# Latent attention with high and low v in one stationary tile, weights divided on GpSimd, scores four tiles ahead, rope rows by DMA and the last product in two parts

## The chip, the cores and the metric

The kernel runs on one core of a Trainium2 chip. The metric is the time of one execution on the device in microseconds (us). A run is timed several times, and the median is given. One further execution is profiled, and every row below comes from it. The engines are TensorE (PE; its weight loads are PEld), VectorE (DVE), ScalarE (ACT), GpSimd (POOL) and SyncE (SP), whose queue issues the DMAs. SBUF is the on-chip memory, PSUM the memory that PE writes its products to.

## The reference

A network of four layers on 512 latent tokens and 256 context tokens of width 1024: Fourier mixing, differential attention, latent attention, Fourier mixing, each followed by an MLP. The change is in the third layer. Cut to what matters there (16 heads, 64 + 32 columns of q and k, 64 of v; 768 keys, and only the 512 latent queries are needed):

```python
def mla_attend(q_nope, q_rope, k_nope, k_rope, v):
    scale = (MLA_NOPE_DIM + MLA_ROPE_DIM) ** -0.5
    s = (einsum("bqhd,bkhd->bhqk", q_nope, k_nope)
         + einsum("bqhr,bkr->bhqk", q_rope, k_rope)) * scale
    p = softmax(s, axis=-1)
    return einsum("bhqk,bkhe->bqhe", p, v)
# mla_mixer: q, k, v by low-rank products of the normed input, the rope part of k shared by all heads,
# q_rope and k_rope rotated; y = concat(heads) @ w_o; x = x + gate * y, then the MLP
```

## The kernel before, in words

All products are made in float32 accuracy from pairs: `split` (L95) rounds a tile to a high part on ACT (L96) and puts the rest, the low part, on DVE (L97); a product is three matmuls, high x high, high x low and low x high (`mm3`, L160). Only PE's order is written by hand: PE executes its instructions in the order of the program text. The other engines' queues are ordered by a scheduler that simulates the program, takes what is ready and prefers what comes first in the text; `tc.high_priority(200)` moves a step forward (the splits of transposed tiles, L799, and the sums into x, L370). Each engine executes its own queue strictly in order. A tile is allocated by a tag with a number of buffers; an instruction that writes a new tile waits until the old tile of its buffer has been read.

The layer (`mla`, L1083) first makes the compressed q and kv (`cqn`, `ckn`), the shared rope rows of k (`krh`, `krl`, 32 rows of 768 columns) and, for four heads at a time, the rope rows of q (`qr_item`, L1180). `kk_rope` (L1170) copies the k rope rows to rows 64 to 96 of one of four key tiles `kkh`, `kkl`; `q_item` (L1220) does the same for the two heads of a pair with the q rope rows (L1230 on ACT, L1231 on DVE).

Then comes a loop over 32 steps c (L1336). A step is 256 queries of one head; eight steps are a group g of four heads. Score tiles are counted by i, two to a step, 128 queries by 768 keys each. `S(i)` (L1269) makes the scores of a tile in six matmuls into a PSUM tile `ps` (tag s, two buffers), takes the row maximum on DVE (L1280), scales it (L1281) and makes the exponential `e` on ACT (L1283; tag e, three buffers). `Tr(i)` (L1286) transposes e on PE, six times 128x128 (L797, in `transpose_g`), into PSUM and splits it to `pth` and `ptl`. `PV(c)` (L1294) multiplies the transposed weights of the step with v in 18 matmuls of 256 columns. Its stationary tile holds 64 columns of v and 64 columns of ones (of zeros for the low part), so that rows of the result hold the sum of the weights; its inverse is made by Ln and Exp on ACT (L1311, L1312), multiplied in on DVE (L1313), and the head's output is split into `oh` and `ol`. The text runs two score tiles ahead: S(0) and S(1), and then in each step Tr(2c), S(2c+2), fill, Tr(2c+1), S(2c+3), fill, PV(c).

`fill` takes other products from a list, about 1.05 us of PE time a call: v of the next group (`v_item`), k and q of the next pair (`k_item`, `q_item`), q rope rows (`qr_item`), and the eight products of the output matrix for the group before (`wo_item`, L1233), each of which ends with a sum into x on DVE (`accum`, L368). Group 3's own eight output products come after the loop, with the steps of the MLP norm behind each (`nm.feed`, L341: a scaled high part on ACT, the low part on DVE, squares on ACT, and a sum `nacc` on POOL, L357). Weights come by `wload` or `gload` on SP's queue into one of two `raw` buffers and are split from there.

Of the kernel before, what the change touches and what calls it, by code (L numbers as in the profile page):

```python
# [44 lines left out]
def body(ctx: ExitStack, tc, a, out):  # L45
# [1037 lines left out]
    def mla(l, h, nm):  # L1083
        T = TT
        with ExitStack() as es:
# [33 lines left out]
            def lat_norm(ps, acc, hl, c0, inv_n, gcol):  # L1119
# [5 lines left out]
                for i, p in enumerate(ps):  # L1125
                    u = qt_("u")[:, :w]
                    nc.vector.scalar_tensor_tensor(u, p, pb[:, gcol + i:gcol + i + 1], r, op0=ALU.mult, op1=ALU.mult)
                    split(hl[i][0][:, c0:c0 + w], hl[i][1][:, c0:c0 + w], u)

            vt = [cp.tile([128, 6, 6, 64], F32R, name=f"vt{q}") for q in range(2)]  # L1130
            zt = sp.tile([128, T], F32, name="zt", tag="e", bufs=3)
            nc.gpsimd.memset(zt[:, :384], 0.0)
            for b in range(2):
                nc.scalar.activation(vt[0][:, :, 3 * b + 1], zt[:, :384].rearrange("p (t e) -> p t e", e=64), AF.Copy, bias=1.0)
                nc.scalar.copy(vt[1][:, :, 3 * b + 1], zt[:, :384].rearrange("p (t e) -> p t e", e=64))
# [11 lines left out]
            lat_norm(pqs, aq, cqn, 0, 1.0 / 256, PB_QG)  # L1147
            akv = sumsq([pkv[:, 0:512]])
            wr = wload(wp, a["mwr"], 256)
            kr = sp.tile([32, T], F32, name="kr", tag="e", bufs=3)  # L1150
            krh, krl = (sp.tile([32, T], F32R, name=n, tag="e", bufs=3) for n in ("krh", "krl"))
# [11 lines left out]
            lat_norm([pkv[:, 0:512]], akv, ckn, 0, 1.0 / 128, PB_KVG)  # L1163
# [6 lines left out]
            def kk_rope():  # L1170
                k_h = hp.tile([96, 776], F32R, name="kkh", tag="h")
                k_l = hp.tile([96, 776], F32R, name="kkl", tag="h")
                nc.scalar.copy(k_h[64:96, :T], rd(krh))
                nc.vector.tensor_copy(k_l[64:96, :T], rd(krl))
# [24 lines left out]
            def v_item(g, t0):  # L1199
# [7 lines left out]
                for b in range(2):  # L1207
                    hi, lo = (q[:, t0:t0 + 2, 2 * b:2 * b + 4:3] for q in vt)
                    split(hi, lo, pv[:, :, 2 * b:2 * b + 2])
# [10 lines left out]
            def q_item(pr):  # L1220
# [3 lines left out]
                for b in range(2):  # L1224
# [5 lines left out]
                    nc.scalar.copy(qh[64:96], rd(qr[hd // 4][0][s]))  # L1230
                    nc.vector.tensor_copy(ql[64:96], rd(qr[hd // 4][1][s]))  # L1231

            def wo_item(g, n, norm=None):  # L1233
                if n == 0:
                    WO[g] = [wload(wp, a["mwo"][2 * g + i]) for i in range(2)]
                p = pt_("u")
                mm3(p, 2, lambda k: kview(WO[g][k], n), lambda k: O[2 * g + k], parts(SL))
                accum(n, 0, SL, p, l, G_A)
                if norm:
                    norm.feed(n)  # L1240
# [28 lines left out]
            def S(i):  # L1269
# [10 lines left out]
                nc.vector.reduce_max(mx, s[:, :T], axis=AX.X)  # L1280
# [195 lines left out]
```

## Time and profile before

| | us |
|---|---|
| median of three runs | 2903.64 |
| lowest and highest of them | 2901.41, 2911.14 |
| the profiled execution | 2903.82 |
| its span, from the first to the last instruction | 2902.0 |
| PE busy in the span | 2756.0 (95%) |
| DVE busy | 1930.2 (67%) |
| ACT busy | 1290.8 (44%) |
| POOL busy | 159.9 (6%) |

The four layers lie behind each other in the span. The loop of the latent attention runs from about 1801 us, where the first row maximum is taken, to 2067 us, where the last PV ends; the output products and the norm follow until about 2090 us. A busy share is the time in which at least one instruction of the engine runs. In rows of groups the number before the arrow is what an instruction writes, the ones behind it what it reads. The granted clock of PE is 0.984 of full speed on average over the span.

### The profile page before, as it was taken

The numbers are of one execution on the slowest core, as the hardware profiler recorded it, in microseconds if no ns is written. First come the engines' busy times: TensorE is split into PE (matmuls) and PEld (weight loads), VectorE is DVE, ScalarE is ACT, GpSimd is POOL, SyncE is SP. The second block draws the span as 40 slices with busy tenths as digits, with TensorE's granted clock in tenths as the row PEclk, the third lists the DMA queues.
The fourth block names the chain that finished last, engine by engine and source line by source line (L and its number), as shares of the span: only waits on it lengthen the run. The fifth ranks groups of instructions, "written<-read, shape, count | busy, mean of one in ns | idle before, by whom it ended". The sixth has DMA issues, their size and how long they took to land.

```text
span 2902.0 us, 39734 instructions
## 1 busy us (share of the span) xinstructions
PE 2756.0 (95%) x15579; PEld 2377.6 (82%) x15579; DVE 1930.2 (67%) x3390; ACT 1290.8 (44%) x2325; POOL 159.9 (6%) x172
## 2 busy tenths in 40 slices
PE   8999999999799989799999998899899999999998
PEld 5788888888788878688888896788788888788887
DVE  7986666558697788875555448888785555664344
ACT  4542222234475656432332236777553334553342
POOL 0110000002110010100000011000100001100001
PEclk9999999999899999999999998999999999999999
DMA  9454333332111111253333210001265551232231
GB/s 319 148 181 131 110 116 104 107 95 82 48 48 45 40 47 39 96 161 114 120 113 116 88 37 32 22 23 37 71 224 175 163 173 55 81 116 95 80 110 51
DMA packets 93531, 291.12 MB, mean 100 GB/s; under 512 B 10624, under 2 KB 14880, under 8 KB 92832
## 3 DMA queue, kind: packets, MB, share of 16 engines
q1 hardware_dynamic: 90784, 285.44, 30.6%
q0 software_dynamic: 2560, 3.15, 0.5%
q8 instruction: 122, 2.00, 0.3%
q14 instruction: 65, 0.53, 0.1%
HBM read 283.29 MB, written 2.11 MB: 98 GB/s over the span
## 4 chain that ended last, share of the span: by engine, by line
PE 79%; DVE 13%; ACT 4%; issue 1%; DMA 1%; POOL 0%; POOLq 0%; SPq 0%; ACTq 0%; DVEq 0%
PE pw L140 70%; PE pu L140 5%; PE ps L140 3%; DVE x L371 2%; PE pu L797 1%; DVE ptl L97 1%; DVE mx L948 1%; DVE wlo L97 1%; DVE hlo L330 1%; DVE nu L328 1%; DVE mx L1280 1%; ACT e L1283 1%; DVE hlo L348 0%; PE pn L140 0%; ACT pth L96 0%
## 5 line engine op out<-in xcount | busy, mean ns | idle before, releaser
L96 ACT CAST whi<-raw 128x1024 fp32r<-128x1024 f32 (+1 forms) x322 | 308.2, 984 | 1064.7 <-PE pw L140 1012.0
L140 PE MATMUL pw<-hhi,wlo 128*128 128x512 f32 (+2 forms) x1680 | 588.0, 350 | 13.0 <-DVE wlo L97 13.0
L140 PE MATMUL pw<-hhi,whi 128*128 128x512 f32 (+2 forms) x1680 | 591.2, 352 | 3.2 <-ACT whi L96 1.5
L140 PE MATMUL pw<-hlo,whi 128*128 128x512 f32 (+2 forms) x1680 | 589.8, 351 | 0.0
L140 PE MATMUL pw<-ahi,whi 128*128 128x512 f32 (+1 forms) x1664 | 569.1, 342 | 0.0
L140 PE MATMUL pw<-alo,whi 128*128 128x512 f32 (+1 forms) x1664 | 567.6, 341 | 0.5 <-DVE alo L97 0.5
L140 PE MATMUL pw<-ahi,wlo 128*128 128x512 f32 (+1 forms) x1664 | 566.6, 340 | 0.0
L371 DVE SCALAR_TENSOR_TENSOR x<-pw,mod,x 128x512 f32<-128x512 f32 (+1 forms) x504 | 302.1, 623 | 283.0 <-PE pw L140 281.8
L97 DVE TENSOR_TENSOR wlo<-raw,whi 128x1024 fp32r<-128x1024 f32 (+1 forms) x322 | 362.2, 1140 | 164.1 <-ACT whi L96 163.5
L140 PEld LDWEIGHTS pw<-hhi,wlo 128*128 128x128 f32 x1680 | 319.4, 190 | 56.7 <-DVE wlo L97 13.6
L140 PEld LDWEIGHTS pw<-hhi,whi 128*128 128x128 f32 x1680 | 318.8, 190 | 47.7 <-ACT whi L96 1.9
L140 PEld LDWEIGHTS pw<-hlo,whi 128*128 128x128 f32 x1680 | 318.7, 190 | 42.4
L140 PEld LDWEIGHTS pw<-ahi,whi 128*128 128x128 f32 x1664 | 315.5, 190 | 37.0 <-issue 0.2
L140 PEld LDWEIGHTS pw<-alo,whi 128*128 128x128 f32 x1664 | 315.5, 190 | 36.2 <-DVE alo L97 0.7
L140 PEld LDWEIGHTS pw<-ahi,wlo 128*128 128x128 f32 x1664 | 315.1, 189 | 36.1
L264 DVE SCALAR_TENSOR_TENSOR raw<-raw,cb 128x1024 f32<-128x1024 f32 x176 | 216.0, 1228 | 117.2 <-DMA raw<-in_modw 115.5
L264 DVE SCALAR_TENSOR_TENSOR junk<-raw,cb 128x1024 bf16<-128x1024 f32 x96 | 117.2, 1220 | 70.6 <-DMA raw<-in_modw 68.4
L97 DVE TENSOR_TENSOR alo<-r,ahi 128x768 fp32r<-128x768 f32 (+2 forms) x134 | 105.8, 792 | 75.1 <-ACT ahi L96 74.8
L307 POOL TENSOR_TENSOR nacc<-nacc,nsq 128x256 f32<-128x256 f32 x70 | 52.9, 755 | 1751.5 <-ACT nsq L306 1751.2
L97 DVE TENSOR_TENSOR ptl<-pu,pth 128x384 fp32r<-128x384 f32 (+1 forms) x208 | 106.2, 539 | 37.5 <-ACT pth L96 36.0
L797 PE MATMUL pu<-ident,e 128*128 128x128 f32 x576 | 89.1, 280 | 21.1 <-ACT e L1283 11.8
L140 PE MATMUL pw<-hhi,g 128*128 128x512 f32 (+2 forms) x384 | 97.8, 337 | 3.9 <-DVE x L371 2.9
(327 smaller groups left out, 4259.4 us busy)
## 6 DMA issues: line engine op xcount, KB each, us to landing
raw<-in_w SPq DMA_DIRECT2D x252, 512.0 KB, 4.1
raw<-in_modw SPq DMA_DIRECT2D x176, 512.0 KB, 3.7
wm<-in_msh SPq DMA_DIRECT2D x32, 256.0 KB, 6.0
raw<-in_fw SPq DMA_DIRECT2D x10, 512.0 KB, 4.3
cb<-scr SPq DMA_DIRECT2D x4, 1024.0 KB, 5.3
raw<-in_dwk SPq DMA_DIRECT2D x16, 256.0 KB, 2.6
raw<-in_dwq SPq DMA_DIRECT2D x16, 256.0 KB, 2.7
raw<-in_dwv SPq DMA_DIRECT2D x16, 256.0 KB, 2.8
```

The costliest lines, as they stand in the source:

```text
L96: nc.scalar.copy(hi, src)
L97: nc.vector.tensor_sub(lo, src, rd(hi))
L140: r = nc.tensor.matmul(o, lhsT, rhs, start=start, stop=stop)
L264: nc.vector.scalar_tensor_tensor(o, m, 1.0, cb[:, v * 1024:(v + 1) * 1024], op0=ALU.mult, op1=ALU.mult, accum_out=mcol(mod[l, ch], v, k))
L307: nc.gpsimd.tensor_tensor(nacc[:, c0:c0 + w], nacc[:, c0:c0 + w], s, op=ALU.add)
L328: nc.vector.scalar_tensor_tensor(u, xs, am, r, op0=ALU.mult, op1=ALU.mult)
L330: nc.vector.scalar_tensor_tensor(lo, u, sh, rd(hi), op0=ALU.add, op1=ALU.subtract)
L371: nc.vector.scalar_tensor_tensor(xs, src, mcol(mod[l, ch], 0 if c0 < SL else 1, n), xs, op0=ALU.mult, op1=ALU.add)
L797: nc.tensor.transpose(t[:, i * 128:(i + 1) * 128], p[:, (k0 + i) * 128:(k0 + i + 1) * 128], ident)
L948: nc.vector.reduce_max(mx, sv, axis=AX.X, negate=True)
L1280: nc.vector.reduce_max(mx, s[:, :T], axis=AX.X)
L1283: nc.scalar.activation(et, s[:, :T], AF.Exp, bias=mx, scale=MLA_SCALE)
```

## The change

- v: the two tiles `vt` (with their columns of ones and zeros) become one tile with v high and v low of a head side by side, 64 columns each, in an order that depends on the head's place in its pair. PV makes 12 matmuls, six with the high and six with the low transposed weights; each gives two sets of 64 rows, one from v high and one from v low. ACT copies one set, and DVE adds the other to it.
- division: the exponential also gives its row sum `li` (`accum_out`), DVE inverts it, and POOL multiplies e by it, in place, before the transposes. The score scale is put into the gain of the compressed q (`qg`), so that the scaling of the maximum goes and the maximum is taken negated.
- scores: four tiles ahead in place of two; tag e has five buffers in place of three. The score tiles keep two PSUM buffers.
- rope rows: the copies to rows 64 to 96 of the q and key tiles become DMAs on SP's queue, forty in all: eight for the keys of four buffers, 32 for the 16 heads.
- last product: in step 30 the list is emptied and the last output weights are loaded and split. After the loop PE makes the first half (heads 12 and 13) of the output products 0 to 3 in the two score buffers, then the last PV, the first half of 4 and 5, and then the second halves, with 6 and 7 whole.

```diff
-                nc.scalar.copy(k_h[64:96, :T], rd(krh))
-                nc.vector.tensor_copy(k_l[64:96, :T], rd(krl))
+                nc.sync.dma_start(rd(k_h)[64:96, :T], rd(krh))
+                nc.sync.dma_start(rd(k_l)[64:96, :T], rd(krl))
...
-                    hi, lo = (q[:, t0:t0 + 2, 2 * b:2 * b + 4:3] for q in vt)
+                    hi, lo = (vt[:, t0:t0 + 2, b::2, q] for q in (b, 1 - b))
...
-                    nc.scalar.copy(qh[64:96], rd(qr[hd // 4][0][s]))
-                    nc.vector.tensor_copy(ql[64:96], rd(qr[hd // 4][1][s]))
-
-            def wo_item(g, n, norm=None):
+                    nc.sync.dma_start(rd(qh)[64:96], rd(qr[hd // 4][0][s]))
+                    nc.sync.dma_start(rd(ql)[64:96], rd(qr[hd // 4][1][s]))
+
+            def wo_load(g):
+                WO[g] = [wload(wp, a["mwo"][2 * g + i]) for i in range(2)]
+
+            def wo_part(p, g, n, k0=0, k1=2):
+                for k in range(k0, k1):
+                    (wh, wl), (oh, ol) = kview(WO[g][k], n), O[2 * g + k]
+                    for i, (u, v) in enumerate(((wh, oh), (wh, ol), (wl, oh))):
+                        mm(p, u, v, k == 0 and i == 0, k == 1 and i == 2)
...
-                nc.vector.reduce_max(mx, s[:, :T], axis=AX.X)
-                nc.vector.tensor_scalar(mx, mx, -MLA_SCALE, None, op0=ALU.mult)
-                et = sp.tile([128, T], F32, name="e", tag="e", bufs=3)
-                nc.scalar.activation(et, s[:, :T], AF.Exp, bias=mx, scale=MLA_SCALE)
+                li = sp.tile([128, 1], F32, name="li", tag="li", bufs=4)
+                nc.vector.reduce_max(mx, s[:, :T], axis=AX.X, negate=True)
+                et = sp.tile([128, T], F32, name="e", tag="e", bufs=5)
+                nc.scalar.activation(et, s[:, :T], AF.Exp, bias=mx, accum_out=li)
+                nc.vector.reciprocal(li, li)
+                nc.gpsimd.tensor_scalar(et, et, li, None, op0=ALU.mult)
...
-                bl = (0, 1, 3, 4)[hd % 4]
-                i = 0
-                for ps in (((vt[0], pth), (vt[1], pth)), ((vt[0], ptl),)):
+                for i, pt in enumerate((pth, ptl)):
                     for kt in range(6):
-                        for vv, pt in ps:
-                            mm(o, vv[:, kt, bl:bl + 2].rearrange("p b e -> p (b e)"), pt[:, kt], i == 0, i == 17)
-                            i += 1
+                        mm(o, vt[:, kt, hd % 4].rearrange("p q e -> p (q e)"), pt[:, kt], i + kt == 0, i + kt == 6)
...
-                nc.scalar.activation(u[s], o[sl], AF.Ln)
-                nc.scalar.activation(u[s], u[s], AF.Exp, scale=-1.0)
-                nc.vector.tensor_mul(u[s], o[s], u[s])
+                nc.scalar.copy(u[s], o[sl])
+                nc.vector.tensor_add(u[s], o[s], u[s])
...
-            st = {0: S(0)}
-            st[1] = S(1)
+            LEAD = 4
+            st = {i: S(i) for i in range(LEAD)}
...
-                    if i + 2 < 2 * NC:
-                        st[i + 2] = S(i + 2)
+                    if i + LEAD < 2 * NC:
+                        st[i + LEAD] = S(i + LEAD)
...
-                PV(c)
+                if c == NC - 2:
+                    while queue:
+                        pop()
+                    wo_load(3)
+                if c < NC - 1:
+                    PV(c)
+
+            ps = []
+            for q in range(2):
+                p = pt_("s")
+                ps.extend((p[:, 0:512], p[:, 512:1024]))
+            for n in range(4):
+                wo_part(ps[n], 3, n, 0, 1)
             ahead_w1(l)
-            while queue:
-                pop()
+            PV(NC - 1)
+            ps.extend(pt_("u") for _ in range(2))
+            for n in range(4, 6):
+                wo_part(ps[n], 3, n, 0, 1)
             for n in range(KT):
-                wo_item(3, n, nm)
+                if n < 6:
+                    wo_part(ps[n], 3, n, 1, 2)
+                else:
+                    ps.append(pt_("u"))
+                    wo_part(ps[n], 3, n)
+                accum(n, 0, SL, ps[n], l, G_A)
+                nm.feed(n)
```

## Rows read from the trace of the kernel before

**Rows 1.** The page, busy us of each engine (share of the span).
```profile
PE 2756.0 (95%) x15579; PEld 2377.6 (82%) x15579; DVE 1930.2 (67%) x3390; ACT 1290.8 (44%) x2325; POOL 159.9 (6%) x172
```

**Rows 2.** Windows: length, then PE, PEld, DVE, ACT, POOL busy (instructions), clock, DMA.
```profile
1801.00:1873.00 72.00, 60.96 (x382) 53.43 (x380) 60.88 (x122) 50.76 (x98) 4.14 (x3) 0.93 0.07 23
1873.00:1939.00 66.00, 64.50 (x427) 57.41 (x428) 54.75 (x111) 48.09 (x97) 0.00 (x0) 1.00 0.05 17
1939.00:2006.00 67.00, 64.62 (x426) 57.18 (x425) 56.78 (x115) 49.43 (x99) 0.00 (x0) 1.00 0.07 24
2006.00:2066.00 60.00, 56.02 (x377) 49.84 (x378) 48.27 (x100) 42.45 (x87) 0.00 (x0) 1.00 0.13 45
...
2075.00:2090.00 15.00, 12.38 (x65) 10.29 (x65) 14.52 (x23) 10.40 (x23) 11.95 (x7) 1.00 0.02 5
```

**Rows 3.** Waits, 1800 to 2090: total us, times, longest.
```profile
ACT e L1283 <- DVE mx L1281: 35.8, 33, 2.1
...
PE pu L797 <- ACT e L1283: 11.8, 9, 2.7
```

**Rows 4.** Chain of work, 2044 to 2095: start, us, what.
```profile
2056.42 1.06 PE ps L140 x6
...
2059.45 2.15 PE pu L140 x18
```

**Rows 5.** Groups of DVE, 1801 to 2066: busy us, mean ns, idle before.
```profile
L97 DVE TENSOR_TENSOR ol<-nu,oh 64x256 fp32r<-64x256 f32 x30 | 12.4, 415 | 0.6
...
L97 DVE TENSOR_TENSOR wlo<-raw,whi 128x1024 fp32r<-128x1024 f32 x6 | 7.2, 1214 | 0.0
...
L1231 DVE CAST ql<-qrl 32x512 fp32r<-32x512 f32 x14 | 5.9, 420 | 0.4
...
L1174 DVE CAST kkl<-krl 32x768 fp32r<-32x768 f32 x2 | 1.1, 552 | 0.1
```

**Rows 6.** Tile nu in the layer: count, ns min/median/max.
```profile
L1312 ACT ACTIVATE nu<-nu x32: 407/416/421, 1817.4 to 2068.2; 64x256 f32<-64x256 f32 x32
```

**Rows 7.** Tile e, accumulator readout in the layer before: count, ns min/median/max.
```profile
L949 ACT ACTIVATION_READ_ACCUMULATOR e<-ps,mx x64: 187/193/219, 762.9 to 1164.1; 128x1 f32 x64
```

**Rows 8.** DVE's waits in the layer before: total us, times, longest.
```profile
DVE li L950 <- ACT e L949: 5.8, 18, 0.9
```

**Rows 9.** Groups of POOL, whole span: busy us, mean ns, idle before.
```profile
L357 POOL TENSOR_TENSOR nacc<-nacc,nsqw 128x768 f32<-128x768 f32 x7 | 16.4, 2350 | 152.7 <-ACT nsqw L356 140.3 <-ACT hhi L96 12.4
L357 POOL TENSOR_TENSOR nacc<-nacc,big 128x768 f32<-128x768 f32 x7 | 13.3, 1895 | 78.4 <-ACT big L356 68.3 <-ACT hhi L96 9.9
...
L839 POOL CAST kl<-big 64x768 fp32r<-64x768 f32 x4 | 3.4, 862 | 0.2
```

**Rows 10.** Timeline of DVE and POOL, 1184 to 1203: start, us.
```profile
1184.70 0.47 DVE L348 SCALAR_TENSOR_TENSOR hlo<-x,am,hhi 128x256 fp32r<-128x256 f32 x1
...
1186.19 2.07 DVE L348 SCALAR_TENSOR_TENSOR hlo<-x,am,hhi 128x256 fp32r<-128x256 f32 x1
...
1186.14 1.84 POOL L357 TENSOR_TENSOR nacc<-nacc,big 128x768 f32<-128x768 f32 x1 [68.09 <-ACT big L356]
```

**Rows 11.** Timeline of DVE and POOL behind the loop: start, us.
```profile
2078.20 0.75 DVE L371 SCALAR_TENSOR_TENSOR x<-pu,mod,x 128x512 f32<-128x512 f32 x1
...
2077.58 12.86 POOL L357 TENSOR_TENSOR nacc<-nacc,nsqw 128x512 f32<-128x512 f32 x7 [243.49 <-ACT hhi L96]
```

**Rows 12.** DMA issues, whole span: count, KB each, us to landing.
```profile
kh<-kh POOLq DMA_DIRECT2D x16, 64.0 KB, 2.3
```

**Rows 13.** Waits of SP's queue, 1700 to 2100: total us, times, longest.
```profile
SPq L116 <- DVE wlo L97: 126.3, 8, 47.0
```

**Rows 14.** Timeline, first transposes: start, us, idle before.
```profile
1804.35 1.54 PE L797 MATMUL pu<-ident,e 128*128 128x128 f32 x6 [2.72 <-ACT e L1283]
```

**Rows 15.** Timeline, last PV and the first sum with the norm: start, us.
```profile
2065.34 1.68 PE L140 MATMUL pu<-pth,vt 128*128 128x256 f32 x12 [0.25 <-ACT pth L96]
...
2074.09 0.75 DVE L371 SCALAR_TENSOR_TENSOR x<-pu,mod,x 128x512 f32<-128x512 f32 x1 [0.59 <-PE pu L140]
```

More of the change, by code (lines that the diff above doesn't have):

```diff
@@ L1126, in lat_norm @@
                     u = qt_("u")[:, :w]
-                    nc.vector.scalar_tensor_tensor(u, p, pb[:, gcol + i:gcol + i + 1], r, op0=ALU.mult, op1=ALU.mult)
+                    nc.vector.scalar_tensor_tensor(u, p, gcol[:, i:i + 1], r, op0=ALU.mult, op1=ALU.mult)
                     split(hl[i][0][:, c0:c0 + w], hl[i][1][:, c0:c0 + w], u)
[L1130 to L1135, printed above, removed]
+            vt = cp.tile([128, 6, 4, 2, 64], F32R, name="vt")
+            qg = cp.tile([128, 2], F32, name="qg")
+            nc.vector.tensor_scalar(qg, pb[:, PB_QG:PB_QG + 2], MLA_SCALE, None, op0=ALU.mult)
             ckn = [[cp.tile([128, T], F32R, name=f"ckn{q}") for q in range(2)]]
@@ L1146, in mla @@
             mm3(pkv, KT, lambda k: kview(wkv, k), hk, [(0, 512)])
-            lat_norm(pqs, aq, cqn, 0, 1.0 / 256, PB_QG)
+            lat_norm(pqs, aq, cqn, 0, 1.0 / 256, qg)
             akv = sumsq([pkv[:, 0:512]])
             wr = wload(wp, a["mwr"], 256)
-            kr = sp.tile([32, T], F32, name="kr", tag="e", bufs=3)
-            krh, krl = (sp.tile([32, T], F32R, name=n, tag="e", bufs=3) for n in ("krh", "krl"))
+            kr = sp.tile([32, T], F32, name="kr", tag="e", bufs=5)
+            krh, krl = (sp.tile([32, T], F32R, name=n, tag="e", bufs=5) for n in ("krh", "krl"))
             def kr_part(c0, w):
@@ L1162, in mla @@
             kr_part(0, 512)
-            lat_norm([pkv[:, 0:512]], akv, ckn, 0, 1.0 / 128, PB_KVG)
+            lat_norm([pkv[:, 0:512]], akv, ckn, 0, 1.0 / 128, pb[:, PB_KVG:])
             pkc = pt_("u")[:, :256]
@@ L1229, in q_item, with wo_item @@
                     s = slice(32 * (hd % 4), 32 * (hd % 4) + 32)
-                    nc.scalar.copy(qh[64:96], rd(qr[hd // 4][0][s]))
-                    nc.vector.tensor_copy(ql[64:96], rd(qr[hd // 4][1][s]))
-            def wo_item(g, n, norm=None):
+                    nc.sync.dma_start(rd(qh)[64:96], rd(qr[hd // 4][0][s]))
[7 more added lines that the diff above has]
+                        mm(p, u, v, k == 0 and i == 0, k == 1 and i == 2)
+            def wo_item(g, n):
                 if n == 0:
-                    WO[g] = [wload(wp, a["mwo"][2 * g + i]) for i in range(2)]
+                    wo_load(g)
                 p = pt_("u")
-                mm3(p, 2, lambda k: kview(WO[g][k], n), lambda k: O[2 * g + k], parts(SL))
+                wo_part(p, g, n)
                 accum(n, 0, SL, p, l, G_A)
-                if norm:
-                    norm.feed(n)
             def v_items(g):
```

2 lines of the change are left out of this document (1 added, 1 removed).

## The prediction

> **What bounds the kernel now.** I began with the page: TensorE (PE) is busy 95% of the span [rows 1], but that is a mean over four layers, and the change touches only the latent attention layer, from about 1801 us (first score tile) to 2090 us (first product of the MLP behind it). So I cut that stretch by the groups of the attention loop: 32 steps c, eight for each group g of four heads [rows 2]. In g=1 and g=2 PE is busy 64.5 of 66 and 64.6 of 67 us, VectorE (DVE) 54.8 and 56.8, ScalarE (ACT) 48 to 49, GpSimd (POOL) nothing: PE is the bound, and DVE is second at 83 to 85%. In g=0 both PE and DVE stand at 61 of 72 us: there the loop waits back and forth between them. In g=3 PE has 56.0 of 60. Behind the loop, in 2075 to 2090, DVE is busy 14.5 of 15 us: the sums and the MLP norm are DVE's. Then the waits: PE waits 11.8 us in nine places for a softmax tile e, and ACT, which makes e, waits 35.8 us for the row maximum from DVE [rows 3]. So two things can be gained: PE time in the steady groups, and DVE time where PE waits for DVE.
>
> **The change part by part.** The sum is made against the profiled execution, 2903.82 us with a span of 2902.0; the median of the three runs, 2903.64, is the same within 0.2.
>
> *High and low v side by side.* Before, each PV ran 18 matmuls of 256 columns in 2.15 us [rows 4], 0.119 us each. Now the stationary tile holds v high in one half and v low in the other, so 12 do. That takes 6 x 0.119 = 0.72 us from each of 32 steps: 22.9 us of PE, 5.7 a group. All of it lies on PE's own queue.
>
> *Division.* Before, a row of ones gave the sum, and each step paid Ln and Exp on ACT and a multiply on DVE. Now a copy takes Ln's place and an add the multiply's, of the same shapes, so I price them alike; the second ACT operation, 0.416 us [rows 6], goes, 32 x 0.416 = 13.3 us of ACT. In exchange each of the 64 exponentials reads out its accumulator, 0.193 us in the layer before [rows 7], 12.4 us of ACT. Zero for ACT, which is not the bound. On DVE a reciprocal of one column replaces the scaling of the maximum, one column too: zero. But it stands behind an exponential on DVE's in-order queue, and the next subtraction for a transposed tile, which PE's PV waits for, is queued behind it. The layer before runs the same pattern, maximum, exponential, reciprocal, and its DVE waited 5.8 us in 18 places [rows 8]: from below zero, from above 6 us, and I leave it to the share that a stretch can reach.
>
> *The multiply on POOL.* No row shows this form. From below, a one-input cast of 768 columns took 0.862 us; from above, two-input adds of 128x768 took 1.895 and 2.350 [rows 9]. It has one tensor input, so I take 1.0 us, near the cast. As latency it fits: POOL gets 64 us of work in 240. Its cost is what it does to DVE. A subtraction of 128x256 with two SBUF inputs took 0.47 us alone and 2.07 us when it started 0.05 us behind a POOL add of 1.84 us: it waited to the end of the POOL operation [rows 10]. A DVE sum that reads PSUM and one SBUF tile took its usual 0.75 us in the middle of seven POOL adds in a row [rows 11]: it was not held. In the loop the maximum and the subtractions of the transposed tiles read PSUM; with two SBUF inputs there are 52 operations (30 ol and 6 wlo [rows 5], two wlo that move in, and by the code 8 g and 6 in the q rope). If POOL is busy 64 x 1.0 / 240 = 27% of the time, each loses 0.27 x 0.5 us on average: 7 us of DVE over the loop, 1.8 a group. By the ends: 0.86 us gives 5 us, 1.9 us gives 26, 2.35 us gives 39.
>
> The Trainium skill ("SBUF — State Buffer", section "Who interferes with whom") says that DVE and GpSimd share a port pair as an exclusive lock: a DVE instruction with two SBUF inputs contends with a GpSimd instruction that reads SBUF, and one with at most one SBUF input, outside the two-port modes, does not. The trace agrees with both halves [rows 10, 11]. It speaks against the division's place: the sum without any lock would be 7 us of DVE smaller.
>
> *Rope rows by DMA.* This takes 14 casts of 0.42 us (ql) and two of 0.55 us (kkl) from DVE in the loop [rows 5], 7 us, and as many from ACT. Forty DMAs go to SP's queue. An SBUF-to-SBUF copy of 64 KB took 2.3 us to land [rows 12]. SP is a queue with long stalls: a weight load there waited up to 47 us for a free raw buffer [rows 13], and anything behind it waits too. I cost the DMAs at zero in the loop: in program order each pair's DMAs stand ahead of the next weight load, their source is ready from the first steps, and each head is asked for two to four score tiles after its q product. If that cover is gone, one pair waits 2.3 us plus what blocks SP. At the start they are exposed: the first rope rows land some 2.3 us after their source, where a copy took 0.6, but DVE and ACT lose the eight casts of the first four heads that stood around it. I take zero there, from -1 to +3.
>
> *Four tiles ahead.* PE issues scores 2 and 3 before the first transpose. But there are still two score buffers in PSUM, so S(i+4) needs the exponential of i+2 to be done. Before, T(i), the transposes of e, needed it two tiles after S(i); now S(i+2) needs it two tiles after S(i) plus one T: the 11.8 us of waits for e can come back as waits for the score buffer. What the lead does buy is room for the accumulator, the reciprocal and POOL behind the exponential, and at the start and the end: PE's 2.72 us idle before the first transpose [rows 14] gets two score tiles' work, and the last tiles no longer wait for an exponential. I give the lead no more than about 1 us at each end.
>
> *Last product in two parts.* The remaining two products of wo2 move into g=3 (12 matmuls of 512 columns, 2.8 us at the 1.06 us that 2304 score columns took [rows 4]); so do the split of the last weights (two wlo of 1.2 us [rows 5]) and two sums of 0.75 us [rows 15] on DVE. Before, from the start of the last PV (2065.34) to the first sum that went through the norm (2074.09) there were 8.75 us [rows 15]. Now: 12 first-part matmuls 2.8 us, of which some 0.5 lie in the wait for the last split; PV 1.43; the chain copy, add, cast, subtraction 1.6 us plus 0.4 of gaps, partly beside two more first parts; the second part 0.7 and a hand-over of 0.3: 6.7 us. I take a gain of 1.7, for the weight split may be late. Behind it the eight sums and norm steps are DVE's 15 us as before.
>
> **The sum by stretch** [rows 2]. For each I take the new busy times and divide the larger by a share that the stretch can reach: 0.96 in g=1 and g=2 (PE has 0.965 to 0.977 now, but DVE will stand closer), 0.95 in g=3, 0.88 in g=0 (0.85 now).
> g=0: PE 61.0 - 5.7 = 55.3; DVE 60.9 - 2.8 (casts) + 1.8 (lock) = 59.9, so 68.1 for 72: -3.9.
> g=1: PE 64.5 - 5.7 = 58.8; DVE 54.8 - 1.7 + 1.8 = 54.9; 61.3 for 66: -4.7.
> g=2: PE 64.6 - 5.7 = 58.9; DVE 56.9; 61.4 for 67: -5.6.
> g=3: PE 56.0 - 5.0 + 2.8 = 53.8; DVE 48.3 - 0.9 + 2.4 + 1.5 + 1.8 = 53.1; 56.6 for 60: -3.4.
> Tail: -1.7. Together -19.3 us: 2903.8 - 19.3 = 2884.5, forecast 2884.
>
> **The rivals.**
> *PE alone decides.* If DVE always has its results ready, the full 22.9 us, most of the 11.8 us of waits and the tail's 1.7 come back, less the 2.8 moved: about -33 us, 2871. For it: PE is over 96% busy in two groups. Against it: DVE at 90% and more beside it.
> *The lock takes half.* If the multiply runs like the two-input add of 1.9 us, DVE gets 26 us for 7, 6.5 a group: 73.4, 62.1, 64.2 and 60.8 us, 4.5 less than before in all, and the tail: -6 us, 2898. For it: POOL's only measured operations of this width and all 128 partitions are the slow ones.
> *Slower by the same lock.* At 2.35 us each, the third POOL row, 9.8 a group come onto DVE: 77.2, 65.5, 67.7 and 64.3 us, +9.7, less the tail 1.7: 2912. It begins to be slower at about 2.1 us a multiply.
> *Rope rows come late.* If a pair's DMAs stand behind a waiting load in SP's order, the loop stops for them: four or five pairs at 2 to 3 us eat half of the gain, 2894. Against it: program order, above.
>
> **How the numbers follow.** A difference of 0.3% (8.7 us) is about what a measurement of this kernel can tell from no change. Chances: forecast 0.55 (2874 to 2895), PE alone 0.15, lock half 0.18, lock slower 0.07, late rope 0.05. Faster than 2895 lie nearly all of the forecast, PE alone, and some of lock half and late rope: 0.73; same 0.17; slower 0.10 (lock slower and the top of lock half). The range leaves out the lower half of PE alone and the slow lock: 2868 to 2902.
>
> **What would show it.** Right: 384 PV matmuls in the layer where 576 were; DVE over 90% busy in g=1 to g=3 and g=0 the longest group; PE's waits for e replaced by waits at the score tiles; POOL multiplies of about 1 us; a few ol and wlo of over 0.8 us; the first sum of the last product some 7 us after the last transposes. Wrong: POOL multiplies near 2 us, ol means over 0.7 us, PE waiting for a DMA into qh or kkh, or DVE clearly under 85% with PE still idle, which would mean that a chain that I priced at zero (accumulator, reciprocal, POOL) sets the pace.

## The result and the profile after

| | before | after |
|---|---|---|
| median, timed side by side (us) | 2904.82 (2901.41 to 2911.14) | 2880.76 (2879.58 to 2881.57) |
| span of the profiled execution (us) | 2902.0 | 2879.8 |

The ratio is 0.9914, with a 95% interval of 0.9899 to 0.9929: 24 us less by the medians, 22.2 by the two profiled spans. The forecast was 2884, with a range of 2868 to 2902.

The page gives the busy times of the engines. PE has 19.6 us and 192 matmuls less than before [rows 1], DVE 5 us less, and POOL 144 us more:

```profile
PE 2736.4 (95%) x15387; PEld 2356.3 (82%) x15387; DVE 1925.4 (67%) x3371; ACT 1269.4 (44%) x2333; POOL 303.9 (11%) x235
```

To see where the time went, both traces are cut at the same events: first score tile, PV(0), PV(8), PV(16), PV(24), the last PV (each by the start of its first matmul), and the statistic of the MLP norm behind the layer. The columns are those of [rows 2]: length, busy time of PE, PEld, DVE, ACT and POOL, PE's granted clock, DMA. First the kernel before:

```profile
1798.50:1813.82 15.32, 12.13 (x50) 10.11 (x49) 10.43 (x22) 10.20 (x20) 0.00 (x0) 0.71 0.01 2
1813.82:1880.15 66.33, 58.42 (x393) 51.65 (x392) 58.01 (x119) 48.55 (x97) 4.14 (x3) 0.97 0.08 25
1880.15:1947.54 67.39, 64.74 (x428) 57.31 (x427) 57.15 (x115) 49.79 (x100) 0.00 (x0) 1.00 0.07 24
1947.54:2014.71 67.17, 64.78 (x429) 57.32 (x428) 56.95 (x115) 49.59 (x99) 0.00 (x0) 1.00 0.07 24
2014.71:2065.34 50.63, 47.88 (x327) 42.94 (x325) 39.19 (x81) 34.29 (x70) 0.00 (x0) 1.00 0.12 43
2065.34:2094.09 28.75, 24.72 (x127) 20.68 (x127) 23.07 (x36) 14.44 (x30) 12.39 (x7) 0.94 0.15 48
```

and the changed kernel:

```profile
1797.57:1813.13 15.56, 14.24 (x62) 11.69 (x61) 10.68 (x22) 10.37 (x23) 10.12 (x5) 0.73 0.20 46
1813.13:1873.06 59.93, 51.17 (x345) 44.85 (x343) 57.09 (x114) 44.02 (x102) 42.13 (x20) 1.00 0.12 35
1873.06:1934.79 61.73, 58.46 (x378) 51.63 (x379) 56.84 (x111) 45.89 (x103) 36.16 (x17) 1.00 0.12 35
1934.79:1996.27 61.48, 58.31 (x380) 51.52 (x379) 56.65 (x111) 45.48 (x103) 36.17 (x17) 1.00 0.16 45
1996.27:2045.33 49.06, 46.07 (x297) 40.59 (x295) 42.09 (x82) 32.36 (x74) 24.84 (x12) 1.00 0.06 20
2045.33:2072.03 26.70, 20.75 (x98) 16.61 (x97) 18.63 (x30) 12.32 (x27) 11.23 (x7) 0.88 0.32 115
```

| stretch | before | after | difference | forecast |
|---|---|---|---|---|
| ahead of the first score tile | 1798.50 | 1797.57 | -0.9 | 0 |
| to PV(0) | 15.32 | 15.56 | +0.2 | 0 |
| PV(0) to PV(8), nearly g=0 | 66.33 | 59.93 | -6.4 | -3.9 |
| PV(8) to PV(16), g=1 | 67.39 | 61.73 | -5.7 | -4.7 |
| PV(16) to PV(24), g=2 | 67.17 | 61.48 | -5.7 | -5.6 |
| PV(24) to the last PV, g=3 | 50.63 | 49.06 | -1.6 | -3.4 |
| last PV to the statistic | 28.75 | 26.70 | -2.0 | -1.7 |
| behind it | 807.91 | 807.77 | -0.1 | 0 |

The forecast's stretches are cut up to some 8 us earlier than these, so a row is compared loosely, the sums strictly: -19.3 forecast, -22.2 found. Of g=0's gain up to 1.7 us is not the change's: before, PE was granted 1.2 GHz for 3.4 us there (the clock column says 0.97), after it was at 2.4 GHz throughout. In the last stretch it is the other way: 1.2 GHz for 3.4 us before and 6.6 us after. At the two ends the rows don't hold the same work: with the new lead the row to PV(0) has two more score tiles and g=3 two fewer. With the lead alone (below) these two rows took 18.74 and 48.45 us. g=1 and g=2 stand at full clock in both and are the clean measure. There PE was busy 96% of the time before and is busy 95% now; DVE went from 85% to 92%.

The waits from 1795 to 2090 us, longest first (total, times, longest). ACT still waits for the maximum [rows 3], PE no longer waits for e at its transposes but at the score tiles, and DVE waits 8.0 us for the accumulator. A wait of PE stands in these rows twice, once for the weight load (PEld) and once for the matmul (PE), so the two are not added: the matmuls waited 6.6 us for e, where before they waited 11.8 [rows 3].

```profile
ACT e L1288 <- DVE mx L1286: 27.6, 32, 1.8
...
PEld ps L140 <- ACT e L1288: 8.4, 7, 1.9
DVE li L1289 <- ACT e L1288: 8.0, 21, 0.6
...
PE ps L140 <- ACT e L1288: 6.6, 6, 1.6
...
PE ps L140 <- DVE x L371: 2.0, 2, 1.2
```

The groups of POOL and DVE in the loop (busy us, mean ns): the multiply takes 2282 ns, more than twice the 1.0 us of the sum, and yet ol, a DVE operation with two SBUF inputs, takes 464 ns on average where it took 415 [rows 5].

```profile
L1290 POOL TENSOR_SCALAR e<-e,li 128x768 f32<-128x768 f32 x64 | 145.6, 2282 | 93.4 <-DVE li L1289 74.5 <-PE pu L140 12.2 <-ACT g L96 3.8
...
L97 DVE TENSOR_TENSOR ol<-nu,oh 64x256 fp32r<-64x256 f32 x30 | 13.9, 464 | 0.4
...
L97 DVE TENSOR_TENSOR wlo<-raw,whi 128x1024 fp32r<-128x1024 f32 x8 | 9.8, 1234 | 0.1
```

The timeline shows why. An ol that started 0.08 us behind a multiply took 1.10 us: it ran 0.42 us from 1921.68 on, so it was let go 0.76 us after the multiply's start, though the multiply went on for another 1.44 us. An ol that started 0.88 us into another multiply took its usual 0.42. Of the 32 ol in the layer only two started in the first 0.76 us of a multiply, and each took 1.10 us; the 20 that started later in one, from 0.88 us on, took 0.40 to 0.47 us. The rows of the two examples:

```profile
1921.00 1.10 DVE L97 TENSOR_TENSOR ol<-nu,oh 64x256 fp32r<-64x256 f32 x1
...
1920.92 2.20 POOL L1290 TENSOR_SCALAR e<-e,li 128x768 f32<-128x768 f32 x1
...
1863.65 0.42 DVE L97 TENSOR_TENSOR ol<-nu,oh 64x256 fp32r<-64x256 f32 x1
...
1862.77 2.21 POOL L1290 TENSOR_SCALAR e<-e,li 128x768 f32<-128x768 f32 x1
```

### The profile page after: what moved, and what is told of

Read it like the earlier page. It is cut to its first block, busy times and chain, and to the rows that moved or that the text cites. A ratio compares the mean times of both kernels' runs of the same rounds, so it can differ in the third digit from the quotient of the medians.

```text
span 2879.8 us, 39661 instructions
## 1 busy us (share of the span) xinstructions
PE 2736.4 (95%) x15387; PEld 2356.3 (82%) x15387; DVE 1925.4 (67%) x3371; ACT 1269.4 (44%) x2333; POOL 303.9 (11%) x235
## 4 chain that ended last, share of the span: by engine, by line
PE 78%; DVE 14%; ACT 4%; DMA 2%; issue 2%; POOL 1%; POOLq 0%; SPq 0%; ACTq 0%; DVEq 0%
PE pw L140 69%; PE pu L140 4%; PE ps L140 3%; DVE x L371 1%; DVE ptl L97 1%; PE pu L797 1%; DVE wlo L97 1%; DVE mx L948 1%; ACT e L1288 1%; DVE mx L1286 1%; DVE nu L328 1%; DVE hlo L330 1%; PE pn L140 0%; DVE hlo L348 0%; DMA raw<-in_w 0%
## 5 line engine op out<-in xcount | busy, mean ns | idle before, releaser
L140 PE MATMUL pw<-hhi,wlo 128*128 128x512 f32 (+2 forms) x1680 | 587.1, 349 | 12.5 <-DVE wlo L97 12.5
L140 PEld LDWEIGHTS pw<-hhi,wlo 128*128 128x128 f32 x1680 | 318.4, 190 | 56.2 <-DVE wlo L97 13.1
L1290 POOL TENSOR_SCALAR e<-e,li 128x768 f32<-128x768 f32 x64 | 145.6, 2282 | 93.4 <-DVE li L1289 74.5
```

Source lines behind the costliest of these rows:

```text
L140: r = nc.tensor.matmul(o, lhsT, rhs, start=start, stop=stop)
L1290: nc.gpsimd.tensor_scalar(et, et, li, None, op0=ALU.mult)
```

## The experiments

Times are medians, with the ratio to the kernel before, which was run on the same chip in the same set, and its 95% interval. Since these differ by up to 0.15% either way, readings of 1 to 5 us go by the stretches of the traces: the changed kernel was run twice with a profile, and PV(8) to PV(16) took 61.73 and 61.77 us, PV(16) to PV(24) 61.48 and 61.52.

### Six matmuls back into each PV

```diff
-                for i, pt in enumerate((pth, ptl)):
+                for i, pt in enumerate((pth, pth, ptl)):
...
-                        mm(o, ..., pt[:, kt], i + kt == 0, i + kt == 6)
+                        mm(o, ..., pt[:, kt], i < 2 and kt == 0, i != 1 and kt == 5)
```

> The changed kernel with six matmuls of 256 columns put back into each PV: the six with the high transposed weights are issued twice, the second time from a fresh start, so the result is the same and PE has 18 matmuls a step as before. Nothing else differs. Theory A (PE sets the pace in the loop, and the gain is the six matmuls): 32 x 0.72 = 22.9 us come back, 2900 to 2906 us, and DVE's busy share in the loop falls from 92% to about 84%. Rival B (DVE, at 92%, or a chain through it sets the pace, and the matmuls lie beside its work): 10 us or less come back, 2881 to 2891 us.

2898.53 us, ratio 0.9973 (0.9963 to 0.9983). Against the second run of the changed kernel (below) 15.6 us by the medians; in the traces, from the first score tile to the statistic, 286.95 us for 274.46: 12.5. (The profiled execution, 2891.61 us, was the fastest of the eight. Its stretch to PV(0) was 1.3 us shorter, with PE at 1.2 GHz for 2.3 us of it, for 8.4 in the changed kernel; from PV(0) on it took 13.8 us more.) g=1 and g=2 of this run:

```profile
1873.25:1938.42 65.17, 63.47 (x426) 57.16 (x427) 56.41 (x111) 45.32 (x103) 35.62 (x17) 1.00 0.12 33
1938.42:2003.59 65.17, 63.47 (x427) 57.15 (x427) 56.41 (x111) 45.27 (x103) 35.62 (x17) 1.00 0.15 43
```

Neither theory: 3.4 and 3.7 us of 5.7 come back. PE is now busy 97% and DVE 87%. PE's busy time rises by 5.1 us a group, less than the 5.7 that the spacing of the matmuls' starts gives. Read from the other end, this kernel has before's matmuls and takes 65.2 us for 67.3: 2.1 us of a group's gain of 5.7 come from the rest of the change, 3.6 from the matmuls. This holds for the six taken away last; the new v alone, in the kernel before, was not tried.

### Score tiles two ahead

```diff
-            LEAD = 4
+            LEAD = 2
```

> The changed kernel with score tiles two ahead in place of four. From the end of a tile's scores the weights need the maximum 0.95, the exponential 0.90, its accumulator 0.20, the reciprocal 0.16 and the multiply 2.21 us, with hand-overs about 4.8 us. At two ahead PE has one transpose, one score tile, a call of fill and half a PV to do in between, about 3.2 us. Theory A (the lead hides the slow multiply): PE waits for POOL some 1.2 to 1.8 us at each of 62 tiles, 75 to 110 us, 2955 to 2990 us. Rival B (with two score buffers PE waits for the exponential in any case, so the lead hides little): within 5 us of the changed kernel, 2878 to 2886 us.

2931.91 us, ratio 1.0086 (1.0071 to 1.0101): 51 us slower than the changed kernel. The waits of its loop (again on the weight loads and on the matmuls), and g=1:

```profile
PEld pu L797 <- POOL e L1290: 53.2, 34, 4.7
...
PE pu L797 <- POOL e L1290: 44.6, 32, 4.5
...
1888.65:1961.38 72.73, 63.04 (x378) 54.40 (x379) 56.61 (x111) 45.91 (x103) 35.05 (x16) 0.95 0.11 30
```

PE waits for POOL at its transposes, of which the changed kernel shows nothing. Theory A, with a smaller price: 11.0 us more in g=1 for 16 tiles, 0.7 us a tile where 1.2 to 1.8 were expected. Part of it is the clock: from PV(0) to the last PV PE was at 1.2 GHz for 40.9 us (6.8 in g=1), in the changed kernel never. By an estimate from these times, half of them at most was lost: up to 20 of the 51 us, and up to 3.4 of the 11.0.

### The lead alone, in the kernel before

```diff
-            st = {0: S(0)}
-            st[1] = S(1)
+            st = {i: S(i) for i in range(4)}
...
-                    if i + 2 < 2 * NC:
-                        st[i + 2] = S(i + 2)
+                    if i + 4 < 2 * NC:
+                        st[i + 4] = S(i + 4)
```

> The kernel before with one part of the change alone: score tiles four ahead, with five buffers for e. Theory A (as predicted: two score buffers tie S(i+2) to the exponential two tiles back, so waits for e come back as waits for a score buffer, and only the start and the end gain): 0 to 3 us less, 2900 to 2904 us. Rival B (the lead by itself frees PE of its waits for e): up to 12 us less, 2892 us.

2906.6 us, ratio 0.9998 (0.9988 to 1.0007): no difference. PV(8) to PV(24) takes 134.4 us for 134.6. The lead by itself is worth nothing in the time; it is the condition under which a multiply of 2.2 us can stand behind the exponential.

### The division with two tensor inputs on POOL

```diff
-                nc.gpsimd.tensor_scalar(et, et, li, None, op0=ALU.mult)
+                nc.gpsimd.tensor_tensor(et, et, li.to_broadcast([128, T]), op=ALU.mult)
```

> The changed kernel with the division on POOL as an operation of two tensors: e times the inverse sums, read as a second input of 768 columns with stride zero. The product is the same. In the trace of the changed kernel a DVE operation with two SBUF inputs that started just behind a POOL multiply was released 0.76 us after the multiply's start; behind a POOL add of two tensors it was 1.65 us, nearly the add's end. Theory A (the lock lasts as long as POOL reads, by its number of inputs): POOL operations of 1.9 to 2.4 us, DVE operations with two SBUF inputs held up to 1.6 us, mean of the 64x256 subtraction ol from 0.46 to 0.7 us or more, and 5 to 20 us more in all, 2886 to 2900 us. Rival B (the lock plays no part in this loop, whatever POOL reads): ol stays under 0.55 us and the time within 3 us of the changed kernel.

2886.74 us, ratio 0.9932 (0.9917 to 0.9947). The multiply became faster, 1516 ns for 2282, and ol slower, 610 ns. An ol 0.05 us behind a multiply took 1.70 us: it was let go at 1840.29, only 0.14 us ahead of the multiply's end:

```profile
L1290 POOL TENSOR_TENSOR e<-e,li 128x768 f32<-128x768 f32 x64 | 96.5, 1516 | 140.4 <-DVE li L1289 107.8 <-PE pu L140 13.3 <-PE pu L797 11.0
...
L97 DVE TENSOR_TENSOR ol<-nu,oh 64x256 fp32r<-64x256 f32 x30 | 18.3, 610 | 0.4
...
1839.01 1.70 DVE L97 TENSOR_TENSOR ol<-nu,oh 64x256 fp32r<-64x256 f32 x1
...
1838.96 1.47 POOL L1290 TENSOR_TENSOR e<-e,li 128x768 f32<-128x768 f32 x1
...
1872.38:1935.15 62.77, 58.44 (x379) 51.63 (x379) 57.96 (x111) 45.93 (x103) 23.91 (x16) 1.00 0.11 34
```

g=1 and g=2 take 1.0 us more each, with 1.1 us more of DVE busy in each; the first score tile to the statistic takes 278.77 for 274.46. The total is at the lower end of theory A, with intervals that overlap those of the changed kernel; the multiply (1.9 to 2.4 expected) and the mean of ol (0.7 or more) came out below it. So a lock that lasts nearly as long as the operation costs about 1 us a group here, though less than theory A said.

### Rope rows by copies again

```diff
-                    nc.sync.dma_start(rd(qh)[64:96], rd(qr[hd // 4][0][s]))
-                    nc.sync.dma_start(rd(ql)[64:96], rd(qr[hd // 4][1][s]))
+                    nc.scalar.copy(qh[64:96], rd(qr[hd // 4][0][s]))
+                    nc.vector.tensor_copy(ql[64:96], rd(qr[hd // 4][1][s]))
```

(and the same for the key rows)

> The changed kernel with the rope rows copied again, high rows on ACT and low rows on DVE, in place of the forty DMAs. Theory A (DVE at 92% of the loop hands PE its inputs, so DVE time counts now): the four casts of 0.42 us that come back to DVE in each of g=1 and g=2 cost 1 to 1.7 us a group, 3 to 6 us in all, 2884 to 2887 us. Rival B (PE sets the pace and the copies lay beside it): within 1.5 us of the changed kernel.

The changed kernel, run again beside this and the next two:

> The changed kernel itself, timed beside the following ones on the same chip so that they have a common measure. Both theories: 2878 to 2884 us, and from PV(8) to PV(24) 123.2 us as in its first profile.

It took 2882.93 us, ratio 0.9921 (0.9906 to 0.9936); the copies 2888.01 us, ratio 0.9936 (0.9921 to 0.9951). The intervals overlap. The stretches to PV(0), g=0, g=1 and g=2 with the copies:

```profile
1798.35:1815.50 17.15, 14.72 (x62) 11.89 (x61) 13.13 (x28) 13.01 (x27) 9.70 (x5) 0.70 0.01 1
1815.50:1878.33 62.83, 53.81 (x344) 46.95 (x342) 57.85 (x117) 47.17 (x106) 42.42 (x20) 0.95 0.07 22
1878.33:1940.96 62.63, 58.57 (x379) 51.58 (x379) 59.21 (x116) 48.49 (x107) 37.54 (x17) 1.00 0.10 30
1940.96:2002.38 61.42, 58.83 (x381) 51.59 (x379) 57.36 (x115) 47.53 (x107) 35.62 (x17) 1.00 0.12 35
```

Against the changed kernel these are +1.6, +2.9, +0.9 and -0.1 us. The 2.9 of g=0 can't be taken as the copies' cost: PE was granted 1.2 GHz for 6.8 us of it here (0.95 in the column) and never in the changed kernel. Of the 1.6 at the start up to 0.9 may be the clock as well (10.2 us at 1.2 GHz for 8.4). What is left is 0.7 to 1.6 us at the start, 0.9 us in g=1 and nothing in g=2. Neither theory holds as stated: the DMAs seem to gain a little, and the exact size stays open.

### The last product whole

```diff
-                if c == NC - 2:
-                    while queue:
-                        pop()
-                    wo_load(3)
-                if c < NC - 1:
-                    PV(c)
...
+                PV(c)
             ahead_w1(l)
...
+            while queue:
+                pop()
             for n in range(KT):
+                wo_item(3, n)
                 nm.feed(n)
```

> The changed kernel with the last output product as before: its weights are loaded after the last PV, and the eight products come whole behind it. Theory A (the division of the last product in two parts takes some 2 us from the stretch behind the last PV and adds the wait for the late weights, 1.2 us, ahead of it): 0.5 to 3 us slower, 2881 to 2884 us, and from the start of the last PV to the statistic of the norm 28 to 29 us where the changed kernel has 26.7. Rival B (the chain of the sums, the norm steps and POOL's sums of squares sets the end whatever the order of the products): that stretch is 26.7 us or less, and the total is the same or lower.

2880.28 us, ratio 0.9916 (0.9899 to 0.9932), beside 0.9921 of the changed kernel: no difference by the medians. The traces, both with 6.6 us at 1.2 GHz in the last stretch, tell more. First this run, PV(24) to the last PV and the last PV to the statistic, then its first sum with the norm (DVE) and its sums of squares (POOL):

```profile
1994.29:2037.32 43.03, 40.84 (x272) 36.14 (x270) 37.28 (x76) 29.69 (x71) 25.17 (x12) 1.00 0.09 27
2037.32:2066.57 29.25, 25.23 (x120) 21.10 (x121) 23.08 (x36) 14.03 (x29) 12.37 (x7) 0.89 0.28 96
...
2045.55 0.75 DVE L371 SCALAR_TENSOR_TENSOR x<-pu,mod,x 128x512 f32<-128x512 f32 x1 [0.59 <-PE pu L140]
...
2049.06 12.84 POOL L357 TENSOR_TENSOR nacc<-nacc,nsqw 128x512 f32<-128x512 f32 x7 [13.10 <-ACT hhi L96]
```

then the changed kernel, the last transposes on PE, the first sum and the sums of squares:

```profile
2042.19 0.44 PE L797 MATMUL pu<-ident,e 128*128 128x128 f32 x2 [1.19 <-DVE ptl L97]
...
2049.52 0.75 DVE L371 SCALAR_TENSOR_TENSOR x<-ps,mod,x 128x512 f32<-128x512 f32 x1 [0.82 <-PE ps L140]
...
2053.84 11.70 POOL L357 TENSOR_TENSOR nacc<-nacc,nsqw 128x512 f32<-128x512 f32 x7 [15.86 <-ACT nsqw L356]
```

The stretch ahead of the last PV is 6.0 us shorter than in the changed kernel (43.03 for 49.06), the one behind it 2.55 longer (29.25 for 26.70): the division in two parts costs 3.5 us net. For the first sum it does what it should: last PV to first sum 4.2 us in place of 8.2. But the twelve first-part matmuls (2.8 us), the two products of wo2 (2.8 us) and the weight splits now stand ahead of the last PV, on PE's path, where the splits hold up the last transposes by 1.19 us. Behind the last PV such work had stood beside DVE's and POOL's: from the first sum on, POOL's seven sums of squares run one behind the other, 12.84 us here and 11.70 there, DVE's norm steps are held beside them (a 128x2 subtraction of 0.15 us took up to 1.23 in the changed kernel), and PE's first MLP products wait for those. And the divided form has a wait of its own, 2.0 us in the rows above (PE ps <- DVE x): the second parts of products 1 and 3, which share a score buffer with 0 and 2, were begun only when the sums of those were done. Theory A is right on the stretch behind the last PV, theory B on the total.

### The low part of the head outputs on POOL

```diff
-                split(oh[s, c0:c0 + 256], ol[s, c0:c0 + 256], u[s])
+                h_, l_ = oh[s, c0:c0 + 256], ol[s, c0:c0 + 256]
+                nc.scalar.copy(h_, u[s])
+                (nc.gpsimd if c < 30 else nc.vector).tensor_tensor(l_, u[s], rd(h_), op=ALU.subtract)
```

> The changed kernel with the low part of the head outputs (the 64x256 subtraction, 0.46 us, 30 of 32) moved from DVE to POOL. DVE loses 3.7 us of 56.8 a group, and its two-input operations with it; POOL gets some 0.8 us each behind its multiplies. Theory A (PE's waits in the loop are DVE's load): PE comes closer to its 58.4 us a group, 1 us or more less in each of g=1 and g=2, 3 to 6 us in all, 2875 to 2878 us. Rival B (PE waits for chains in a fixed order, not for DVE's load): within 1.5 us of the changed kernel; slower if POOL's queue delays the multiplies.

2875.65 us, ratio 0.9898 (0.9884 to 0.9913). g=1 and g=2, and the group of the moved subtraction:

```profile
1870.84:1930.17 59.33, 58.08 (x379) 51.67 (x379) 52.96 (x103) 45.20 (x103) 41.27 (x26) 1.00 0.13 37
1930.17:1989.48 59.31, 58.08 (x378) 51.67 (x378) 52.95 (x103) 45.22 (x103) 40.88 (x25) 1.00 0.17 49
...
L1318 POOL TENSOR_TENSOR ol<-nu,oh 64x256 fp32r<-64x256 f32 x30 | 23.0, 765 | 15.0 <-ACT oh L1317 14.0
```

2.4 and 2.2 us less a group, with PE 98% busy and DVE 89%. PE's matmuls are the same. Theory A: in the changed kernel time on DVE, 3.9 us a group less here, kept PE from its work. The lock on ol, which goes too, is too small for it (1.5 us in the whole loop). Whether DVE's load as such counts, or only the place of ol in its queue, this edit can't tell apart. The other stretches are within 0.3 us of the changed kernel, but for the one to PV(0), 1.3 us shorter with PE at 1.2 GHz for 2.0 us in place of 8.4.

### The two improvements together

The last two edits in one kernel.

> The changed kernel with the low part of the head outputs on POOL, and with the last output product whole behind the last PV. Theory A (the two act in different stretches, the first in g=1 and g=2, the second in g=3 and behind): the loop gives 6.3 + 3.5 = 9.8 us less in the profile than the changed kernel, 2870 to 2873 us. Rival B (both take the same slack of DVE): only the larger of the two, 2875 to 2877 us.

2870.25 us, ratio 0.9873 (0.9859 to 0.9888): the fastest of all. In the trace the first score tile to the statistic takes 264.78 us, 9.7 less than in the changed kernel; the two alone gave 6.2 and 3.4. Of the 9.7 and of the 6.2, 1.3 lie ahead of PV(0), where the clock differed as in the run before; from PV(0) on the gains are 8.4, 4.9 and 3.4 us. Theory A: they add up. Its g=1:

```profile
1872.06:1931.40 59.34, 58.07 (x378) 51.67 (x378) 52.94 (x103) 45.26 (x103) 41.24 (x26) 1.00 0.14 37
```

The same with the two-input division:

> As the run with the head outputs' low part on POOL and the last product whole, and with the division on POOL as an operation of two tensors (1.47 us, but it held the DVE subtraction ol up to its end). Theory A (the 1.0 us a group that the two-input form cost was the lock on ol, and ol is now off DVE): g=1 and g=2 take 59.3 us as without it, total within 1.5 us of that run. Rival B (the cost lay elsewhere): g=1 and g=2 again take about 1 us more, 60.3 us, and the total is 3 to 5 us above it.

2873.78 us, ratio 0.9880 (0.9862 to 0.9899).

```profile
1877.23:1936.54 59.31, 58.05 (x378) 51.65 (x379) 52.94 (x103) 45.25 (x103) 29.21 (x24) 1.00 0.13 37
1936.54:1995.87 59.33, 58.05 (x378) 51.65 (x378) 52.95 (x103) 45.28 (x104) 29.19 (x24) 1.00 0.13 37
```

g=1 and g=2 are the 59.3 us of the run without it: the 1.0 us a group is gone once ol is off DVE. Theory A there. That it was the lock on ol fits the row of ol above (0.15 us more on seven or eight a group); but DVE has more spare time here, in which a hold of another operation would not show. The median is 3.5 us higher, as rival B had it, but the intervals overlap and the two can't be told apart; g=0 took 4.3 us more in the profile, with PE at 1.2 GHz for 13.7 us of it, against 3.4.

And with the six matmuls put back:

> As the run with the head outputs' low part on POOL and the last product whole, with the six matmuls put back into each PV. Theory A (a group takes PE's time or what DVE allows, whichever is more; with DVE at 89% of 59.3 us PE alone decides): each group takes the full 5.7 us more, 65.0 us in g=1 and g=2, total 2892 to 2896 us. Rival B (part of PV's matmuls lies beside other work in any case): 3.6 us a group as with the full DVE load, 62.9 us.

2886.11 us, ratio 0.9933 (0.9916 to 0.9950).

```profile
1872.27:1936.13 63.86, 63.23 (x426) 57.11 (x427) 53.60 (x103) 45.23 (x103) 40.27 (x24) 1.00 0.12 34
1936.13:1999.79 63.66, 63.11 (x429) 57.03 (x427) 53.48 (x103) 45.19 (x103) 40.98 (x25) 1.00 0.12 34
```

4.4 us a group, between the theories: more than the 3.6 with DVE at 92%, less than 5.7. PE's busy time rose by 5.1 us a group, as in the first experiment, and its idle time fell from 1.3 to 0.6: even with DVE at 89% some of the matmuls' time fits into gaps of PE.

### The prices on POOL

Three operations of each form on a tile of their own, ahead of the loop; DVE ran products of two 128x64 tiles meanwhile.

```diff
+                        nc.gpsimd.tensor_scalar(j1, j1, lj, None, op0=ALU.mult)
...
+                        nc.gpsimd.tensor_scalar(j1, j1, 1.0, None, op0=ALU.mult)
...
+                        nc.gpsimd.tensor_tensor(j1, j1, lj.to_broadcast([128, T]), op=ALU.mult)
...
+                        nc.gpsimd.tensor_tensor(j1, j1, j2, op=ALU.mult)
```

> The changed kernel with operations put in ahead of the latent attention loop, to read their durations only; the time of the whole is not to be compared. Four forms on POOL, 128x768 in float32, three of each: a multiply by a column of inverse sums, a multiply by a constant, a multiply with a second input of stride zero, a multiply of two full tiles; meanwhile DVE runs products of two 128x64 SBUF tiles. Theory A (the one-input form is slow in itself, and DVE is locked out only for the 768 reads at its start): column and constant both 2.2 us, one DVE operation beside each held about 0.7 us and the others not; the two-input forms 1.5 to 1.9 us, DVE held to the end. Rival B (the column makes it slow): the constant takes about 0.9 us.

The groups (L1328 by a constant, L1332 two tiles, L1330 a stride of zero), two of DVE's products and the multiply by a constant beside them:

```profile
L1328 POOL TENSOR_SCALAR pja<-pja 128x768 f32<-128x768 f32 x3 | 6.4, 2129 | 0.3
L1332 POOL TENSOR_TENSOR pja<-pja,pjb 128x768 f32<-128x768 f32 x3 | 5.4, 1799 | 0.2
L1330 POOL TENSOR_TENSOR pja<-pja,pjl 128x768 f32<-128x768 f32 x3 | 4.4, 1465 | 0.2
...
1794.37 0.78 DVE L1334 TENSOR_TENSOR pjc<-pjc,pjd 128x64 f32<-128x64 f32 x1
...
1795.41 0.21 DVE L1334 TENSOR_TENSOR pjc<-pjc,pjd 128x64 f32<-128x64 f32 x1
...
1794.25 2.13 POOL L1328 TENSOR_SCALAR pja<-pja 128x768 f32<-128x768 f32 x1
```

By a constant 2129 ns. By the column 2340 at the least, but DVE's operations held these three; in the loop of the changed kernel the median is 2207. So the one-input form is slow in itself, column or not. Two full tiles took 1799, a second input of stride zero 1465. DVE's product, usually 0.21 us, took 0.78 when it started 0.12 us into the multiply, and 0.21 when it started 1.16 us into it: again let go some 0.7 us after the start. No DVE product came to lie beside these two-input forms. One lay beside another two-input POOL operation of this run, a rope product (L1099) of 1.26 us: it started 0.10 us into it at 1864.34 and took 1.25 us, so it was held to about 0.1 us before the end, like the ol of the run above.

## Why the prediction was right, and where it was not

The time and its mechanism were right in the main: 384 PV matmuls for 576, and a gain of nearly the size of those matmuls. By its steps:

*Six matmuls less a step: 22.9 us.* As PE work this held (0.71 us for six matmuls, by the starts of the remaining ones; PE's busy time on the page fell by 19.6). As time on the path it was too large: with DVE at 92% only 3.6 of 5.7 us a group return when the six are put back. The sum came out near the time because it divided by shares that a stretch can reach, and because the other parts gave 2.1 us a group, which the prediction had at nearly nothing. That these make up for each other is in part luck. Which of them did is only partly shown: the lead alone gives none, the rope DMAs at most 0.9 us a group; the division with its lead wasn't tried without the new v, so its share is open.

*The multiply: 1.0 us.* Wrong by a factor of two; it took 2.28. I placed it by the one-input cast of 0.862 us, as "near the cast", and the upper bound of 2.35 was the nearer one [rows 9]; the cast had 64 partitions and another operation. By the prediction's own point, slower than before from 2.1 us a multiply, the kernel should have lost, and "POOL multiplies near 2 us" stands among its signs of being wrong.

*The lock: 7 us of DVE, 39 at 2.35 us.* By the multiply it was 1.6: 1.5 on ol (30 x 0.049) and 0.1 on wlo. (Another 1.0 fell on one low part of the q rope, 1.65 us for 0.68 at 1824.66, behind POOL's two-input rope product.) The step that failed is that an operation holds DVE as long as it runs, read from one pair with a two-input add [rows 10]. A one-input multiply held DVE for the first 0.76 us of its 2.2. The two errors worked against each other: 0.76 us of lock is near the 1.0 us that the sum used. By its own formula that would still be 4 us of DVE; that it was less is the order of the queues, in which two of 32 ol met the first 0.76 us of a multiply, where starts spread evenly would have met it six or seven times (an estimate: 64 x 0.76 of 240 us, for 32 ol). None of this was foreseen: here the forecast was lucky. So the two rivals that hung on the multiply's time (2898 and 2912) had their condition met, and not their consequence. (In the sum of the first, 1.9 us a multiply gives 25 us of lock by the same formula, not 26; nothing hangs on it.)

The Trainium skill ("SBUF — State Buffer", section "Who interferes with whom") calls the lock exclusive, for a DVE instruction with two SBUF inputs against a GpSimd instruction that reads SBUF. The two-input division agrees (1.70 us for ol, to 0.14 us of the end); the one-input multiply agrees only for its first third.

*Lead: no gain in itself, waits for e come back at the score buffers.* Right: PE's matmuls wait 6.6 us at ps, where they waited 11.8 at the transposes before, and there was no difference when the lead was made alone (7.9 us of waits at ps there). What the text valued too little is the other side: with two tiles ahead the changed kernel is 51 us slower, the lower clock included. It stood there as "room" with no number.

*Rope rows: zero in the loop, -1 to +3 us at the start.* No wait of PE for one of these DMAs appeared, as said. But they seem to gain a little, 0.7 to 1.6 us at the start, where DVE was busy 13.1 us with the copies and 10.7 without, and at most 0.9 us a group.

*Division.* DVE's waits for the accumulator, 8.0 us in 21 places, are above the 6 us that the text gave as the bound. What they cost in time no run shows.

*Last product.* The first sum came 7.3 us after the last transposes (2042.19 to 2049.52), for 6.7. But its gain of 1.7 us and its cost of 2.8 us in g=3 were added as if they were alike; the parts themselves made a small loss of it, and it was 3.5 us: g=3 and the tail gained 3.6 us, for 5.1 (up to 1.6 of the difference can be the tail's lower clock). What was missed is that PE work behind the last PV had a cover, the sums and POOL's sums of squares, and ahead of it has none, and that the second parts wait for the sums of their neighbours.

*Shares.* DVE over 90% held in g=1 and g=2 (92%), not in g=3 (86%). g=0 was not the longest group: 59.9 us for 61.7. Its DVE reached 95%, more than the 0.88 that the sum allowed.

## What to carry to other kernels

Where one engine is at 95% and a second at 92%, work taken off the first returns only in part, and moving some of the second engine's work elsewhere returns more: here a subtraction of 0.46 us, given to POOL, was worth 2.3 us in each of the two clean groups. A slow operation on an engine that had been idle cost little here once the order of issue ran far enough ahead of it; price its latency against the lead, not its busy time. Before work is moved ahead of the last step, ask what covered it where it stood.

## What the runs showed of the hardware that was not expected

- A POOL multiply of one 128x768 float32 tile by a column or a constant took 2.1 to 2.3 us, one of two tiles 1.80, and one whose second input is a column with stride zero 1.47: of these forms the ones with one tensor input are the slowest.
- DVE operations with two SBUF inputs (the 32 ol of the changed kernel) were held if they started in the first 0.76 us of a one-input POOL multiply of 2.2 us (two of two) and not from 0.88 us on (none of 20); behind a two-input one of 1.47 us an ol was held to 0.14 us before its end. The other way round a POOL multiply that started 0.25 us into a wlo of 1.21 us took 3.03 us in place of 2.21.
